# A new order of heads and filler in the mixer of a two-layer encoder, values by token tile, and inverse roots by one polynomial

## The chip, the cores and the metric

The kernel runs on one core of a Trainium2 chip. The metric is device time in microseconds (us) of one execution. Three runs of the kernel before took 1954.21, 1957.28 and 1953.86 us; the median is 1954.21 us.

## The reference

A trunk of two layers works on one sequence of 512 tokens with 1024 features. Each layer is a half-step SwiGLU, a token mixer, and another half-step SwiGLU; each is entered through an RMS norm with a learned shift and scale, and added to the residual through a gate. The change lies in the mixer (and in the helper for inverse roots, which all norms use):

```python
def token_mixing(h, cos, sin, w_in, sink, onorm_a, onorm_b, w_out):
    qa, ka, va, qb, kb, vb = jnp.split(h @ w_in, IN_SPLITS, axis=-1)
    qa, ka, qb, kb = (apply_rope(t, cos, sin) for t in (qa, ka, qb, kb))
    oa, _ = banded_attention(qa, ka, va, 128, sink)       # 8 heads, 2 key/value heads, |i-j| <= 128
    for window, dilation in ((128, 1), (512, 4), (2048, 16)):
        o, l = dilated_branch(qb, kb, vb, window, dilation)   # 8 heads, merged by their denominators
        ...
    ya = rmsnorm(oa, onorm_a)
    yb = rmsnorm(ob, onorm_b)
    return jnp.concatenate([ya, yb], axis=-1) @ w_out
```

All is float32, and the kernel keeps that precision: each operand is held as a high part and a low part, and a product is three TensorE matmuls (high by high, high by low, low by high).

## The kernel before, in words

Features lie on the 128 partitions and the 512 tokens in the free dimension. Weights come in chunks of 128x1024 (512 KB): `emit_chunk` loads one (L148), ScalarE makes its high part (L152) and VectorE its low part (L153). `chunk` hands over the next chunk, and `ahead` keeps three loaded beyond it.

**Sixteen heads.** The mixer has 8 heads of kind B (masked, all 512 keys for each tile of 128 queries) and 8 of kind A (a band, 256 or 384 keys). Two heads are a pair, since they share one 128-row projection. b0 to b3 and a0 to a3 are the pairs. Every pair has its own query projection; each B pair has its own keys, and all A pairs share one key projection, `ka`. Values of all heads are made in two halves of 320 columns by `vproj`.

**A head's work.** `scores(qt)` makes a tile of scores with two matmuls (L690, L691), adds the mask and takes the row extreme on VectorE (L695), and takes the exponential on ScalarE (L699). The result is a buffer `sm`, of which there are five. `pv(kt)` transposes one key tile of the probabilities on TensorE (L724), makes high and low parts (L727 on ScalarE, L728 on VectorE) and multiplies by the values (L731, L732) into the PSUM tile `po`. `finish` brings `po` to SBUF (L741 ScalarE, L742 VectorE); for the second head of a pair it also transposes the denominators (L746, tile `pd`), multiplies them in (L747) and adds the squares for the branch's norm. `heads_` goes through the heads: while it does the four `pv` of one head it issues the four `scores` of the next, so a head is four steps and a fifth for `finish`. Five steps stand ahead of the first head.

**Filler.** `weave` draws other TensorE work into these steps. Before the change the filler is first `fill_b`: both halves of the values, then nine projections (`proj`: 24 matmuls of 512 columns, then `rope`) in the order q, k of b2, q, k of b3, ka, and the four qa. Each step draws 1.62 us of it (FB; in the code's own reckoning a projection is 5.2 us and half of the values 13.1 us). Head 10 and later draw 0.45 us per step (FA) from `fill_a`: the conversion of the four normed B tiles (`conv`, L792 to L794) and the B half of the output projection (eight jobs of 12 matmuls, each with a residual addition, L391). What is left of a filler is drawn at its end.

**`rope`** reads a projection's PSUM tile twice on VectorE (L605, L606), goes through GpSimd (L607), adds (L608), makes the high part on ScalarE (L609) and the low part on GpSimd (L611), and moves the result into place with four DMAs for a query and eight for a key, all in SP's queue. Its temporaries `part`, `t1` and `qh` have one buffer each, so the next `rope` has to wait until these DMAs have read them. Queries go to `qs` (two buffers), keys to `kh` and `kl` (two buffers each).

**PSUM** has eight tiles of 128x512: four of tag `mm` (projections, values, `po`, `pd`), two for scores, two of tag `pt` (transposes, statistics).

**The norm of branch B.** `bb.stat` sums the squares of the B heads on TensorE (L774) and takes the inverse root on VectorE (`rsqrt`, L232 to L238: ten small operations, each on the one before). `bb.bcast` spreads the root by four transposes (`pRo`, L782) and a copy (L786); the filler `fill_a` needs it. HJ places `stat` at the first step of head 9 and `bcast` at its fourth. The norm of branch A follows all heads.

**Order on the engines.** The program is traced in the order told here, and the framework that builds it orders each engine's instructions once, at build time, by readiness and a priority that goes by place in the trace. `high_priority(offset=...)` moves an instruction ahead by so many places: heads by 50 (HB) up to head 7, by 150 (HA) after. That order is part of the program.

Of the kernel before, what the change touches and what calls it, by code (L numbers as in the profile page):

```python
# [1 line left out]

# [15 lines left out]
L = 2  # L18
# [13 lines left out]
RA, RB, RQ = 10.0 / 3, 5.0, 9.0 / 64  # L32
RK = (8.0 / 3) ** 12
# [14 lines left out]
HJ = [(9, 0), (9, 3)]  # L48
HN = 10
# [5 lines left out]
FB = 1.62  # L55
FA = 0.45
# [7 lines left out]
def tile_trunk(ctx: ExitStack, tc: tile.TileContext, xT, c, positions, adaT, cols, sink, wi1, wo1,  # L64
# [44 lines left out]
    for l in range(L):  # L109
        for sub, (wi, wo) in enumerate(((wi1, wo1), (None, None), (wi2, wo2))):  # L110
            finer.update(range(len(specs) - 3, len(specs) + 6))
            if wi is None:
                for j in (0, 1, 2, 3):
                    specs.append(wqk[l, j])
                for a in range(2):
                    for k0, n in ((0, 3), (3, 3), (6, 2)):
                        specs.append(wv[l, a][:, k0 * 320:(k0 + n) * 320])
                for j in range(4, 13):
                    specs.append(wqk[l, j])
# [472 lines left out]
    def mixer(l, norm, pool, mod):  # L592
# [8 lines left out]
        def rope(p, kind):  # L601
# [12 lines left out]
            if kind == "q":  # L614
# [7 lines left out]
            kh = pool.tile([128, 2, S], F32R, tag="kh", name="kh", bufs=2)  # L622
            kl = pool.tile([128, 2, S], F32R, tag="kl", name="kl", bufs=2)
# [7 lines left out]
        def proj(kind, dst):  # L631
# [5 lines left out]
            dst.append(rope(p, kind))  # L637
            ahead()

        def vproj():  # L640
            for _ in range(4):
                V2.append(pool.tile([128, 10, 2, 64], F32R, tag=f"v{len(V2)}", name="v2"))
            for a in range(2):
                ps = [pm.tile([128, S], F32, tag="mm", name="mm") for _ in range(4)]
                for k0, n in ((0, 3), (3, 3), (6, 2)):
                    W = chunk()
                    for tt in range(4):
                        for j in range(n):
                            k = k0 + j
                            ts = slice(tt * 128, tt * 128 + 128)  # L650
                            o = ps[tt][:, :320]
                            wh, wl = (w[:, j * 320:(j + 1) * 320] for w in W)
                            hh, hl = norm.h[k]
                            T.matmul(o, hh[:, ts], wh, start=k == 0, stop=False)  # L654
                            T.matmul(o, hh[:, ts], wl, start=False, stop=False)
                            T.matmul(o, hl[:, ts], wh, start=False, stop=k == KD - 1)
                            yield 0.41
                    ahead()
                for tt in range(4):
                    src = ps[tt][:, :320].rearrange("p (h d) -> p h d", d=64)  # L660
                    dst = V2[tt][:, 5 * a:5 * a + 5]
                    with tc.high_priority(offset=HP):
                        A.activation(dst[:, :, 0, :], src, AF.Copy)
                        V.tensor_tensor(dst[:, :, 1, :], src, V2[tt].bitcast(F32)[:, 5 * a:5 * a + 5, 0, :],
                                        op=ALU.subtract)
                vdone.append(a)

        two, halves = [], []

        class Head:  # L670
# [160 lines left out]
        def weave(main, fills):  # L831

            due = 0.0
            i = 0
            for n in main:
                if i + 1 < len(fills) and n >= fills[i + 1][0]:
                    for _ in fills[i][1]:
                        pass
                    i += 1
                    due = 0.0  # L840
                due += fills[i][2]
                while due > 0:
                    d = next(fills[i][1], None)
                    if d is None:
                        break
                    due -= d
            for _ in fills[i][1]:
                pass

        kinds = "qkqk"  # L850
        st = []
        for j, p in enumerate(group(norm, gs, sh, 4)):
            st.append(rope(p, kinds[j]))
        def fill_b():
            yield from vproj()
            for kind in "qkqkkqqqq":
                yield from proj(kind, st)
# [3 lines left out]
        def need(n):  # L861
            while len(st) < n:
                next(fb)

        def head_b(i, a):
            def f():
                need(2 * i + 2)
# [309 lines left out]
```

## Time and profile before

| | us |
|---|---|
| median of 3 runs | 1954.21 |
| lowest and highest | 1953.86, 1957.28 |
| the profiled execution, its own time | 1957.33 |
| its span, from first to last instruction | 1955.5 |
| TensorE busy | 1910.5 (98%) |
| VectorE busy | 1521.8 (78%) |
| ScalarE busy | 943.0 (48%) |
| mean granted TensorE clock | 0.993 |

The span is what the trace covers; the execution's own time has 1.8 us around it. A busy TensorE is not one at its peak, since ends of matmuls are modelled, so where its speed matters the spacing of starts is read. The two mixers lie at about 380 to 650 us and 1330 to 1600 us.

### The profile page before, as it was taken

To read this page: it belongs to the slowest core of one execution; us is meant where nothing else is said; L and a number is where in the kernel's file an instruction comes from. 1 tells how busy PE (TensorE), PEld (TensorE's weight loads), DVE (VectorE), ACT (ScalarE), POOL (GpSimd) and SP (SyncE) were. 2 spreads that over 40 slices of the span, in tenths; PEclk is the share of its full clock that TensorE was granted. 3 is DMA by queue.
4 is the path that set the end of the run, shared out by engine and by line. 5 is a ranking of instruction groups with operands and counts; after the bars stand their busy time and mean duration, and the time that the engine had idled before them with its cause. 6 is when DMAs were issued, how large, how long until landed. Compare 5 with 4: busy or idle time off the path is not lost.

```text
span 1955.5 us, 31018 instructions
## 1 busy us (share of the span) xinstructions
PE 1910.5 (98%) x12000; PEld 1713.5 (88%) x12000; DVE 1521.8 (78%) x2687; ACT 943.0 (48%) x1782; POOL 86.5 (4%) x63
## 2 busy tenths in 40 slices
PE   7999999999989999999999999999999999999998
PEld 5788888898768998989999898999977799898998
DVE  8868384477888988899688898867778889686773
ACT  5422222246665553536446363553657656353552
POOL 2000000011210000000000000000222000000000
PEclk8999999999989999999999999999999999999999
DMA  7778384244521155463414645342543113333231
GB/s 273 281 270 308 122 290 152 76 127 124 129 66 54 55 165 196 147 206 129 150 58 151 204 135 167 108 130 73 157 114 103 38 50 106 100 105 120 80 117 44
DMA packets 84678, 267.96 MB, mean 137 GB/s; under 512 B 10673, under 2 KB 13361, under 8 KB 84530
## 3 DMA queue, kind: packets, MB, share of 16 engines
q1 hardware_dynamic: 84530, 265.98, 42.5%
q8 instruction: 94, 1.54, 0.3%
q14 instruction: 54, 0.44, 0.1%
HBM read 244.97 MB, written 2.10 MB: 126 GB/s over the span
## 4 chain that ended last, share of the span: by engine, by line
PE 86%; DVE 6%; ACT 3%; DMA 2%; issue 2%; POOL 0%; SPq 0%; DVEq 0%; ACTq 0%; POOLq 0%
PE mm L221 16%; PE mm L222 16%; PE mm L223 16%; PE mm L483 9%; PE mm L484 9%; PE mm L485 9%; PE ptr L724 2%; PE po L731 1%; DVE araw L315 1%; PE po L732 1%; DMA araw<-in_adaT_dram 1%; PE s L690 1%; PE s L691 1%; ACT sm L699 1%; PE mm L654 1%
## 5 line engine op out<-in xcount | busy, mean ns | idle before, releaser
L152 ACT ACTIVATE hi<-raw 128x512 fp32r<-128x512 f32 (+5 forms) x253 | 215.1, 865 | 296.9 <-PE mm L223 204.0
L153 DVE TENSOR_TENSOR lo<-raw,hi 128x512 fp32r<-128x512 f32 (+5 forms) x253 | 258.7, 1032 | 88.0 <-ACT hi L152 86.7
L221 PE MATMUL mm<-hh,hi 128*128 128x512 f32 (+1 forms) x864 | 306.6, 356 | 8.0 <-ACT hh L293 7.7
L223 PE MATMUL mm<-hl,hi 128*128 128x512 f32 (+1 forms) x864 | 303.0, 356 | 2.9 <-DVE hl L294 2.9
L222 PE MATMUL mm<-hh,lo 128*128 128x512 f32 (+1 forms) x864 | 305.3, 355 | 0.5 <-DVE lo L990 0.4
L222 PE MATMUL mm<-gh,lo 128*128 128x512 f32 (+1 forms) x832 | 297.0, 357 | 0.0
L221 PE MATMUL mm<-gh,hi 128*128 128x512 f32 (+1 forms) x832 | 296.8, 357 | 0.0
L223 PE MATMUL mm<-gl,hi 128*128 128x512 f32 (+1 forms) x832 | 296.5, 356 | 0.0
L483 PE MATMUL mm<-sh,hi 128*128 128x256 f32 x912 | 260.2, 285 | 1.2 <-ACT sc L505 0.7
L484 PE MATMUL mm<-sh,lo 128*128 128x256 f32 x912 | 258.2, 283 | 0.0
L485 PE MATMUL mm<-sl,hi 128*128 128x256 f32 x912 | 258.0, 283 | 0.0
L180 ACT ACTIVATE hi<-raw 128x512 fp32r<-128x512 f32 x228 | 132.3, 623 | 141.4 <-issue 73.4
L221 PEld LDWEIGHTS mm<-hh,hi 128*128 128x128 f32 x864 | 164.2, 190 | 30.8 <-ACT hh L293 9.4
L391 DVE SCALAR_TENSOR_TENSOR x<-mm,fin,x 128x512 f32<-128x512 f32 (+1 forms) x156 | 101.7, 654 | 112.4 <-PE mm L223 112.0
L223 PEld LDWEIGHTS mm<-hl,hi 128*128 128x128 f32 x864 | 163.1, 190 | 26.2 <-DVE hl L294 5.1
L222 PEld LDWEIGHTS mm<-hh,lo 128*128 128x128 f32 x864 | 163.8, 190 | 22.6 <-DVE lo L990 1.8
L223 PEld LDWEIGHTS mm<-gl,hi 128*128 128x128 f32 x832 | 157.2, 189 | 22.6
L222 PEld LDWEIGHTS mm<-gh,lo 128*128 128x128 f32 x832 | 157.3, 189 | 22.3
L221 PEld LDWEIGHTS mm<-gh,hi 128*128 128x128 f32 x832 | 157.2, 189 | 22.2
L483 PEld LDWEIGHTS mm<-sh,hi 128*128 128x128 f32 x912 | 173.9, 191 | 2.0 <-ACT sc L505 0.9
L484 PEld LDWEIGHTS mm<-sh,lo 128*128 128x128 f32 x912 | 174.2, 191 | 0.0
L485 PEld LDWEIGHTS mm<-sl,hi 128*128 128x128 f32 x912 | 174.1, 191 | 0.0
(185 smaller groups left out, 4016.4 us busy)
## 6 DMA issues: line engine op xcount, KB each, us to landing
raw<-in_wi_dram SPq DMA_DIRECT2D x171, 512.0 KB, 3.7
araw<-in_adaT_dram SPq DMA_DIRECT2D x144, 512.0 KB, 4.6
raw<-in_wo_dram SPq DMA_DIRECT2D x64, 448.0 KB, 3.9
raw<-in_wo_dram SPq DMA_DIRECT2D x32, 512.0 KB, 3.6
raw<-in_wqk_dram SPq DMA_DIRECT2D x26, 512.0 KB, 3.9
raw<-in_w_out_dram SPq DMA_DIRECT2D x16, 512.0 KB, 3.7
kh<-qh SPq DMA_DIRECT2D x40, 128.0 KB, 2.3
kl<-t SPq DMA_DIRECT2D x40, 128.0 KB, 2.3
```

Of the source, the lines that this page charges most:

```text
L152: A.activation(hi[:, sl], raw[:, sl], AF.Copy)
L153: V.tensor_tensor(lo[:, sl], raw[:, sl], hi.bitcast(F32)[:, sl], op=ALU.subtract)
L180: A.activation(d, r, AF.Copy)
L221: T.matmul(ps, wh, X[0][:, s], start=start, stop=False)
L222: T.matmul(ps, wl, X[0][:, s], start=False, stop=False)
L223: T.matmul(ps, wh, X[1][:, s], start=False, stop=stop)
L315: return V.tensor_tensor_reduce(out=raw, in0=raw, in1=by, scale=1.0, scalar=0.0, op0=ALU.mult, op1=ALU.add, accum_out=mod[:, l, ch, k:k + ...
L391: ins = V.scalar_tensor_tensor(x[:, m, s], ps[:, s], gate[:, m:m + 1], x[:, m, s], op0=ALU.mult, op1=ALU.add).ins
L483: T.matmul(ps, wh, xh, start=start and k == 0, stop=False, skip_group_check=True)
L484: T.matmul(ps, wl, xh, start=False, stop=False, skip_group_check=True)
L485: T.matmul(ps, wh, xl, start=False, stop=stop and k == 3, skip_group_check=True)
L724: T.transpose(p[:, j * 128:j * 128 + 128], self.sm[qt][:, c0:c0 + 128], ident)
```

## The change

Heads come in the order b0 b1 a0 b2 b3 a1 a2 a3. The filler is one chain: half 0 of the values, ka, qa0, qb2, kb2, half 1 of the values, qb3, kb3, qa1, qa2, qa3, and behind them `fill_a`, which yields nothing to do until `bb.R` is there. A step draws 2.7 us up to head 5, 0.75 us from head 6, 0.85 us from head 10. `stat` moves to the last step of head 10 and `bcast` to the third step of head 11. A half of the values is made token tile by token tile, in one PSUM tile at a time, with its three chunks fetched at its start; the columns of the weights are regrouped so that half 0 serves b0, b1 and a0. Keys have one buffer of each of two tags instead of two of one: kb0 and ka share the first, kb1, kb2 and kb3 the second. HB holds up to head 9. `rsqrt` has one cubic polynomial instead of two steps: eight operations instead of ten.

```diff
+PAIRS = ("b0", "b1", "a0", "b2", "b3", "a1", "a2", "a3")
+FILL = ("v0", "ka", "qa0", "qb2", "kb2", "v1", "qb3", "kb3", "qa1", "qa2", "qa3")
-HJ = [(9, 0), (9, 3)]
-HN = 10
+HJ = [(10, 3), (11, 2)]
+RATES = ((0, 2.7), (6, 0.75), (10, 0.85))
-FB = 1.62
-FA = 0.45
...
-        for ca, cb, o in ((RA, RB, y), (RA / RQ, RB / RQ ** 2, out)):
-            V.tensor_tensor(t, y, y, op=ALU.mult)
-            V.tensor_tensor(t, t, v, op=ALU.mult)
-            V.scalar_tensor_tensor(q, t, -ca, t, op0=ALU.add, op1=ALU.mult)
-            last = V.scalar_tensor_tensor(o, q, cb, y, op0=ALU.add, op1=ALU.mult).ins
+        V.tensor_tensor(t, y, y, op=ALU.mult)
+        V.tensor_tensor(t, t, v, op=ALU.mult)
+        for i, ca in enumerate(RC):
+            o, u = (out, y) if i == 3 else (q, t)
+            last = V.scalar_tensor_tensor(o, q if i else t, ca, u, op0=ALU.add, op1=ALU.mult).ins
...
-            kh = pool.tile([128, 2, S], F32R, tag="kh", name="kh", bufs=2)
-            kl = pool.tile([128, 2, S], F32R, tag="kl", name="kl", bufs=2)
+            j = kind in ("kb1", "kb2", "kb3")
+            kh = pool.tile([128, 2, S], F32R, tag=f"kh{j:d}", name="kh")
+            kl = pool.tile([128, 2, S], F32R, tag=f"kl{j:d}", name="kl")
...
+        def vproj(a):
+            Ws = []
+            for k0, n in VK:
+                W = chunk()
+                Ws += [(W, j) for j in range(n)]
+            for tt in range(4):
+                p = pm.tile([128, S], F32, tag="mm", name="mm")
+                for k, (W, j) in enumerate(Ws):
...
+                vdone.append((a, tt))
...
             def pv(self, kt):
+                while (self.vh // 5, kt) not in vdone:
+                    next(fb)
                 if kt == 0:
-                    while len(vdone) < self.vh // 5 + 1:
-                        next(fb)
...
-                with tc.high_priority(offset=hp[0] if n < 8 else hp[1]):
+                with tc.high_priority(offset=hp[0] if n < 10 else hp[1]):
...
         def fill_a():
+            while not hasattr(bb, "R"):
+                yield None
...
+        weave(heads([head(t, a) for t in PAIRS for a in range(2)], (HB, HA), {HJ[0]: bb.stat, HJ[1]: bb.bcast}),
+              chain(fb, fill_a()), RATES)
```

## Rows read from the trace of the kernel before

**Rows 1.** The page: busy time of TensorE, share, instructions.

```profile
PE 1910.5 (98%) x12000; PEld 1713.5 (88%) x12000; DVE 1521.8 (78%) x2687; ACT 943.0 (48%) x1782; POOL 86.5 (4%) x63
```

**Rows 2.** Stretches of layer 0's mixer: us, busy PE, PEld, DVE, ACT, POOL, clock, DMA.

```profile
430.00:556.00 126.00, 124.74 (x666) 102.34 (x665) 100.75 (x205) 82.82 (x171) 26.32 (x19) 1.00 0.42 116
556.00:568.00 12.00, 5.66 (x37) 4.43 (x37) 11.05 (x32) 7.27 (x19) 3.05 (x2) 0.90 0.11 27
568.00:576.00 8.00, 8.00 (x30) 6.84 (x31) 4.78 (x14) 3.94 (x10) 0.00 (x0) 0.50 0.39 110
576.00:600.00 24.00, 21.62 (x121) 16.55 (x120) 21.40 (x66) 21.14 (x63) 0.00 (x0) 1.00 0.03 7
```

**Rows 3.** The same view of layer 1's mixer, around its stall.

```profile
1505.00:1518.00 13.00, 6.66 (x42) 5.27 (x41) 11.36 (x33) 7.85 (x19) 3.12 (x3) 0.87 0.17 41
1518.00:1522.00 4.00, 4.00 (x17) 3.13 (x17) 2.14 (x5) 1.94 (x5) 0.00 (x0) 0.57 0.36 122
```

**Rows 4.** Timeline, TensorE: start, us, engine, line, instruction, idle before it.

```profile
567.91 0.45 PE L782 MATMUL pRo<-ident,y 128*128 128x128 f32 x1 [6.03 <-DVE y L238]
```

**Rows 5.** Timeline, VectorE, in the same stall.

```profile
564.48 0.69 DVE L153 TENSOR_TENSOR lo<-raw,hi 128x512 fp32r<-128x512 f32 x1
...
567.41 0.16 DVE L237 SCALAR_TENSOR_TENSOR r<-r 128x4 f32<-128x4 f32 x1
567.61 0.16 DVE L238 SCALAR_TENSOR_TENSOR y<-r,r 128x4 f32<-128x4 f32 x1
```

**Rows 6.** Timeline, ScalarE: ends of A heads behind the stall.

```profile
576.10 0.59 ACT L741 ACTIVATE y<-po 64x512 f32<-64x512 f32 x1 [1.05 <-PE po L732]
...
593.00 0.59 ACT L741 ACTIVATE y<-po 64x512 f32<-64x512 f32 x1
```

**Rows 7.** Timeline, TensorE: first matmuls of the values and of branch A's output.

```profile
419.95 0.31 PE L654 MATMUL mm<-hi,hh 128*128 128x320 f32 x1
...
623.84 0.39 PE L221 MATMUL mm<-yah,hi 128*128 128x512 f32 x1
```

**Rows 8.** Dense stretches, columns as rows 2: 256-column and 512-column matmuls.

```profile
1640.00:1650.00 10.00, 10.00 (x86) 10.00 (x85) 10.00 (x16) 6.37 (x13) 0.00 (x0) 1.00 0.41 119
1690.00:1700.00 10.00, 10.00 (x46) 8.29 (x45) 6.24 (x9) 2.32 (x5) 0.00 (x0) 1.00 0.29 94
```

**Rows 9.** Timeline, TensorE: eight transposes of probabilities in a row.

```profile
541.33 1.04 PE L724 MATMUL ptr<-ident,sm 128*128 128x128 f32 x8
```

**Rows 10.** VectorE groups by shape, 418 to 616 us: count, busy us, mean ns, idle.

```profile
L695 DVE CUSTOM_DVE_ANT_0 sm<-s,mask 128x512 f32<-128x512 f32 x32 | 21.5, 687 | 5.2 <-PE s L691 4.9
L728 DVE TENSOR_TENSOR pl<-ptr,ph 128x512 fp32r<-128x512 f32 x32 | 21.3, 685 | 3.1 <-ACT ph L727 2.9
L742 DVE TENSOR_TENSOR y<-po,y 64x512 f32<-64x512 f32 x16 | 11.0, 688 | 6.4 <-ACT y L741 6.2
L695 DVE CUSTOM_DVE_ANT_0 sm<-s,mask,nsnk 128x384 f32<-128x384 f32 x16 | 9.6, 611 | 0.2 <-PE ptr L724 0.2
L605 DVE STREAM_SHUFFLE part<-mm 128x512 f32<-128x512 f32 x12 | 8.9, 745 | 0.0
L728 DVE TENSOR_TENSOR pl<-ptr,ph 128x384 fp32r<-128x384 f32 x16 | 8.8, 549 | 1.8 <-ACT ph L727 1.7
L608 DVE TENSOR_TENSOR t<-t,part 128x512 f32<-128x512 f32 x12 | 8.2, 686 | 0.2
...
L695 DVE CUSTOM_DVE_ANT_0 sm<-s,mask,nsnk 128x256 f32<-128x256 f32 x16 | 7.3, 478 | 0.6 <-PE s L691 0.5
L728 DVE TENSOR_TENSOR pl<-ptr,ph 128x256 fp32r<-128x256 f32 x16 | 6.7, 417 | 2.9 <-ACT ph L727 2.8
```

**Rows 11.** ScalarE groups by shape, same stretch.

```profile
L699 ACT ACTIVATE sm<-sm,nb 128x512 f32<-128x512 f32 x32 | 23.0, 719 | 13.3 <-DVE nb L695 13.3
L727 ACT ACTIVATE ph<-ptr 128x512 fp32r<-128x512 f32 x32 | 18.3, 594 | 6.1 <-PE ptr L724 5.7
...
L699 ACT ACTIVATION_READ_ACCUMULATOR sm<-sm,nb 128x1 f32 x64 | 12.1, 189 | 0.0
```

More of the change, by code (lines that the diff above doesn't have):

```diff
@@ L1 @@
 from contextlib import ExitStack, nullcontext
+from itertools import chain
 import numpy as np
@@ L112, in tile_trunk @@
             if wi is None:
[L113 to L119, printed above, removed]
+                specs += [wqk[l, QK.index(t)] for t in FIRST]
+                for t in FILL:
+                    if t[0] == "v":
+                        for k0, n in VK:
+                            specs.append(wv[l, int(t[1])][:, k0 * 320:(k0 + n) * 320])
+                    else:
+                        specs.append(wqk[l, QK.index(t)])
                 for half in (1, 0):
@@ L629, in rope, with proj @@
             return kh, kl
-        def proj(kind, dst):
+        def proj(kind):
             W = chunk()
@@ L636, in proj @@
                 yield 0.65
-            dst.append(rope(p, kind))
+            st[kind] = rope(p, kind)
             ahead()
[L640 to L657, printed above, removed]
-                    ahead()
[L659 to L666, printed above, removed]
@@ L668, in mixer @@
-        two, halves = [], []
+        def vproj(a):
+            if not V2:
+                V2.extend(pool.tile([128, 10, 2, 64], F32R, tag=f"v{tt}", name="v2") for tt in range(4))
+            Ws = []
+            for k0, n in VK:
+                W = chunk()
+                Ws += [(W, j) for j in range(n)]
+            for tt in range(4):
+                ts = slice(tt * 128, tt * 128 + 128)
+                p = pm.tile([128, S], F32, tag="mm", name="mm")
+                o = p[:, :320]
+                for k, (W, j) in enumerate(Ws):
+                    wh, wl = (w[:, j * 320:(j + 1) * 320] for w in W)
+                    hh, hl = norm.h[k]
+                    T.matmul(o, hh[:, ts], wh, start=k == 0, stop=False)
+                    T.matmul(o, hh[:, ts], wl, start=False, stop=False)
+                    T.matmul(o, hl[:, ts], wh, start=False, stop=k == KD - 1)
+                    yield 0.44
+                src = o.rearrange("p (h d) -> p h d", d=64)
+                dst = V2[tt][:, 5 * a:5 * a + 5]
+                with tc.high_priority(offset=HP):
+                    A.activation(dst[:, :, 0, :], src, AF.Copy)
+                    V.tensor_tensor(dst[:, :, 1, :], src, V2[tt].bitcast(F32)[:, 5 * a:5 * a + 5, 0, :],
+                                    op=ALU.subtract)
+                vdone.append((a, tt))
+                if tt < 3:
+                    ahead()
+            ahead()
@@ L670, in mixer @@
+        two = []
         class Head:
@@ L829, in heads_, with weave, head @@
                 cur = nxt
-        def weave(main, fills):
+        def weave(main, fill, rates):
             due = 0.0
-            i = 0
             for n in main:
[L836 to L841, printed above, removed]
+                due += [r for h, r in rates if n >= h][-1]
                 while due > 0:
-                    d = next(fills[i][1], None)
+                    d = next(fill, None)
                     if d is None:
+                        due = 0.0
                         break
                     due -= d
-            for _ in fills[i][1]:
+            for _ in fill:
                 pass
[L850 to L853, printed above, removed]
+        st = {}
+        for t, p in zip(FIRST, group(norm, gs, sh, 4)):
+            st[t] = rope(p, t)
         def fill_b():
-            yield from vproj()
-            for kind in "qkqkkqqqq":
-                yield from proj(kind, st)
+            for t in FILL:
+                yield from vproj(int(t[1])) if t[0] == "v" else proj(t)
         fb = fill_b()
[L861 to L865, printed above, removed]
+        def head(t, a):
             def f():
-                need(2 * i + 2)
-                return Head(st[2 * i], a, st[2 * i + 1], a, 2 + 2 * i + a, bb, False, None)
+                i = int(t[1])
+                h = 2 * i + a
+                kind, vh = ("kb%d" % i, h + h // 4) if t[0] == "b" else ("ka", 4 + 5 * (i // 2))
+                for need in ("q" + t, kind):
+                    while need not in st:
+                        next(fb)
+                if t[0] == "b":
+                    return Head(st["q" + t], a, st[kind], a, vh, bb, False, None)
+                return Head(st["q" + t], a, st[kind], i // 2, vh, ba, True, l * 8 + h)
             return f
@@ L914, in fill_a @@
                 ahead()
-        weave(heads([head_b(i, a) for i in range(4) for a in range(2)] +
-                    [head_a(i, a) for i in range(4) for a in range(2)], (HB, HA), {HJ[0]: bb.stat, HJ[1]: bb.bcast}),
-              ((0, fb, FB), (HN, fill_a(), FA)))
+        weave(heads([head(t, a) for t in PAIRS for a in range(2)], (HB, HA), {HJ[0]: bb.stat, HJ[1]: bb.bcast}),
+              chain(fb, fill_a()), RATES)
         nxt = Norm()
```

22 lines of the change are left out of this document (11 added, 11 removed).

## The prediction

> **What bounds the kernel now.** I read the page first, then the stretches of the two mixers, then the timeline at the one deep gap, then the groups by shape. The page [rows 1] says that TensorE is busy 98% of the span: a change in order can win only where TensorE waits, or runs slowly, inside the mixers. The stretches of layer 0 [rows 2] show where. From 430 to 556 us, while heads and filler run together, TensorE is busy 124.7 of 126 us and VectorE 100.8: TensorE bounds. From 556 to 568 TensorE is busy 5.7 of 12 us, and the next 8 us run at a granted clock of 0.50 (1.2 of 2.4 GHz). From 576 to 600 only heads run and little filler: VectorE is busy 21.4 of 24 us (89%), so VectorE bounds here, and TensorE waits in small pieces. Layer 1 repeats this with about 4 us at a clock of 0.57 [rows 3].
>
> The timeline names the deep gap: TensorE stood 6.03 us in front of `pRo`, the spreading of the B norm's root [rows 4]. VectorE was not idle; it did the root's small operations between 0.69 us ones of the backlog [rows 5]. In that order nothing behind `pRo` can go ahead.
>
> Behind the gap, the end of one A head and that of the third one after it lie 16.9 us apart [rows 6]: **5.63 us for an A head without much filler.**
>
> **The change part by part.** I price the stage from the first matmul of the values, 419.95 us, to the first of branch A's output, 623.84 us [rows 7]: 203.9 us in layer 0.
>
> *TensorE's prices.* Dense stretches give 10/86 = 0.116 us for a matmul of 256 columns and 10/46 = 0.217 for 512 [rows 8]; between them 0.142 for 320 and 0.167 for 384 columns are estimates on that line. A transpose is 1.04/8 = 0.13 us [rows 9]. So a projection (24 matmuls) is 5.2 us, both halves of the values (192) 27.2, a B head (16 matmuls of 512, 18 transposes) 5.8, an A head (8 of 384, 8 of 256, 12 transposes) 3.8, and the B half of the output projection (96) 20.9. Before, the filled part lasted from 419.95 to about 556.6 us and held the values, nine projections, eight B heads and two A heads: 27.2 + 46.8 + 46.4 + 7.6 = 128 us of work in 136.7, a factor of 1.07 that I keep.
>
> *Order and rates.* The old rate draws 73 us of filler (in the code's reckoning) at 1.62 a step, 5 of them early for the first `pv`; it is used up near step 42, in the last B head. The new one draws 75 us at 2.7 a step: used up at step 28, in the first head of a0. Nothing more can be drawn until `bcast` at step 63, since `fill_a` waits for the root; the rate of 0.75 draws nothing. I split the stage there.
>
> - Part one, filled: values 27.2, eight of the nine projections 41.6 (the ninth has no PSUM tile until a rope is freed), four B heads 23.2, half an A head 1.9 and scores of the next 0.6: 94.5 x 1.07 = **101 us**, bound by TensorE.
> - Part two, steps 28 to 63: three A heads' worth and the four B heads b2, b3, bound by VectorE. An A head is 5.63. A B head has more VectorE work: four score tiles at 687 and four low parts at 685 ns against two each at 611, 478, 549 and 417 [rows 10], 5.49 less 4.11 = 1.38 us, so 7.0. Its bounds: below, TensorE's own 5.8 x 1.07 = 6.2; above, 7.9, the chain through the five `sm` buffers. In a B head all four `sm` are read until the last `pv`, so three of the next head's scores can only follow: 3 x 0.687, an exponential of 0.719 + 0.189 [rows 11], four transposes 0.5, a high part 0.594, two low parts 1.37, four transposes 0.5, the `finish` addition 0.69 [rows 10], and 0.2 at each of six changes of engine (an estimate, from the 0.2 us between dependent small operations, rows 5), 7.8 to 7.9. I take 7.0, nearest the measured pace of heads. Four ropes fall here too, 0.745 + 2 x 0.686 = 2.1 us of VectorE each, 8.5; bounds 0 (in TensorE's shade) and 8.5; I take 8.5, as VectorE bounds. 16.9 + 28.0 + 8.5 = **53.4 us.**
> - Part three: four and a half A heads 17.2, the output projection 20.9, two statistics of some 32 transposes and one-column matmuls 4.2: 42.3 x 1.07 = **45 us**, bound by TensorE; VectorE has some 25 us of heads and 16 of conversions and additions beside it.
>
> Sum 199.4, so 4.5 us less than 203.9. In layer 1 the old stage lost 1.7 us to the half clock (0.43 of 4) against 4.0 (0.50 of 8), so 2.2 us less there. Together **-6.7 us.**
>
> For the split of regimes the stretches show 100.8 of 126 us of VectorE in the filled part and 21.4 of 24 in the unfilled one [rows 2]. The Trainium skill (Perfetto Trace Analysis, Optimization Strategy) advises to interleave regimes in which different engines are contended. By it a filler drawn sooner lengthens the unmixed part and gives nothing, so that only the roots below would be won; by my rows the mix of the third part pays for the second.
>
> *The stall.* `stat` to `bcast` was three steps and is seven, some 9 us of heads, against the 6.03 us missed [rows 4]. I cost the wait at nothing because these heads hide it. If that cover is gone the price is 6 us a layer. VectorE stays late then, in any case.
>
> *Roots.* Two operations less, 0.2 us apart [rows 5]: 0.4 us each, on the path at the kernel's first norm and its last, **-0.8 us**; the others lie beside matmuls. They also end 0.4 us sooner at `pRo`, within the cover above.
>
> *Values by token tile.* The same 192 matmuls, eight additions and ScalarE copies. Its three chunks must be there within the first 18 matmuls, 2.5 us, instead of 10; `ahead` has loaded them beside the four first projections. Bounds 0 and 2.5 us a layer; I take 0. The gain, that `pv` waits for one tile, has its worth in part one, which TensorE bounds: 0.
>
> *Keys' buffers, and SP's queue.* The number of DMAs is the same. The keys of b3 now wait for the last scores of b2, at step 39, and hold `t1` and `qh`; three projections wait behind them in three of the four `mm` tiles, and `po` and `pd` share the last one. Queued behind: ropes on VectorE, and on SP the copies of qa1. What waits for these is a1, three heads later. Bounds 0 and four hand-overs of the last PSUM tile, 0.59 [rows 6] + 0.69 [rows 10] = 1.28 us each, 5.1 a layer; I take 0, since most of it would fall where VectorE has other work. The regrouped weights cost nothing on the chip.
>
> Total -7.5 us. The profiled execution took 1957.33 us, its span of 1955.5 and 1.8 around it; it becomes 1949.8. The profiled one is 3.1 above the median of 1954.21, so against the median the same difference gives **1947 us**.
>
> **The rivals.** *One, slower: buffers bind in part two.* From step 28 on, B heads run at the `sm` chain's 7.9 us and each `po` waits for the last PSUM tile. 4 x 0.9 + 5.1 = 8.7 us a layer, 17.4 in all: 1964 us. It outweighs the gain from 3.7 us a layer on, and makes the kernel measurably slower from 5.7. For it: nothing in the trace shows a B head without filler, and three held tiles follow from the code. Against it: A heads kept VectorE 89% busy [rows 2]. The same page of the Trainium skill and section says that repeated equal gaps on the engine that should be full can mean that SBUF or PSUM has no room for the next tile; that is this rival, and by it the time is the one just given. No gap of that kind is in the trace before.
>
> *Two: the stall comes back.* The order is fixed at build time, and VectorE is again behind it when `pRo` stands in TensorE's line. 2 x 6.0 us: 1959 us. For it: VectorE is the later engine all through part two. Against it: four steps more.
>
> *Three: more is won.* The ropes of part two hide after all: 8.5 us a layer, 1930 us. For it: VectorE's sums count operations that overlap at their edges. Against it: VectorE at 89%.
>
> **How the numbers follow.** My forecast has 0.42, rival one 0.28, two 0.13, three 0.17. A measurement of this kernel can tell about 0.2%, 3.9 us, from no change. Faster by more: 0.85 of the forecast's share (its takings of 0 could eat 4 us) and all of three, 0.53. Within: the rest of the forecast, a fifth of one and under half of two, 0.17. Slower: 0.30. Cases of both signs hold much; the forecast's own range is 1940 to 1952 (part two's B heads at 6.2 or 7.6). The range of 1930 to 1966 reaches to rivals three and one; what lies beyond either is under 2 in 10.
>
> **What would show it.** Right: no wait over 2 us of `pRo` for VectorE; no stretch at a clock of 0.5 in the mixers; filler's `mm<-hh` matmuls gone some 105 us into the stage; then about 53 us with TensorE some 80% and VectorE 90% busy; the stage at 199 us. Rival one: TensorE and VectorE both below 85% there, and ends of B heads about 8 us apart or more. Rival two: `pRo` with an idle of 4 us or more. I would be wrong altogether if the filler's end stays near 130 us into the stage, for then the rates do not set its place, or if the time changes outside the mixers.

## The result, and the profile after

The changed kernel takes 1967.95 us (median of four runs, 1966.8 to 1969.93) against 1954.03 us: a ratio of 1.0069, with a 95% interval of 1.0051 to 1.0086. It is slower, where a gain of 7.5 us had been forecast, and the time lies 2 us above the upper end of the range.

The page of the profile has TensorE's busy share as before, 98% [rows 1]; the two VectorE operations less in each root show in VectorE's count, 2,653 for 2,687:

```profile
PE 1920.0 (98%) x12000; PEld 1716.6 (87%) x12000; DVE 1517.0 (77%) x2653; ACT 940.7 (48%) x1782; POOL 87.2 (4%) x63
```

The stage that the prediction priced runs, in layer 0, between these two rows of TensorE's timeline (they answer to [rows 7]): 210.9 us where it was 203.9.

```profile
418.05 0.31 PE L661 MATMUL mm<-hi,hh 128*128 128x320 f32 x1
...
628.94 0.50 PE L226 MATMUL mm<-yah,hi 128*128 128x512 f32 x1 [0.35 <-ACT yah L801]
```

In layer 1 it grew by 9.4 us, from 201.2 (1370.9 to 1572.0) to 210.5 (1374.1 to 1584.7). The first of the two stages starts 1.9 us earlier than before, and what lies between them takes another 1.8 us less, so that the end of the second comes 12.6 us later: all but 0.1 of what the spans differ by (1968.2 against 1955.5). Nothing is lost outside the mixers.

Now the stage, cut at the same places in both kernels: its first 20 us, then to the last filler matmul of high part by high part (`mm<-hh,hi`), then to `pRo`, then to the end. The view of stretches, columns as in [rows 2]; first the kernel before:

```profile
419.90:439.90 20.00, 19.27 (x124) 17.92 (x123) 10.57 (x23) 9.15 (x18) 5.83 (x5) 1.00 0.54 158
439.90:555.60 115.70, 114.44 (x601) 92.73 (x600) 93.65 (x190) 75.08 (x156) 24.21 (x18) 1.00 0.45 123
555.60:568.00 12.40, 6.06 (x39) 4.79 (x38) 11.05 (x32) 7.67 (x19) 3.05 (x2) 0.91 0.14 33
568.00:623.80 55.80, 53.39 (x274) 43.05 (x275) 45.06 (x118) 36.10 (x93) 0.00 (x0) 0.93 0.16 47
```

and the changed kernel, with its layer 1 between filler and `pRo` as the last row:

```profile
418.00:438.00 20.00, 20.00 (x127) 18.70 (x126) 13.21 (x26) 10.57 (x21) 5.53 (x5) 1.00 0.59 153
438.00:537.00 99.00, 97.15 (x507) 79.45 (x506) 70.49 (x143) 54.89 (x113) 20.97 (x14) 1.00 0.43 123
537.00:583.00 46.00, 37.49 (x174) 26.49 (x172) 37.85 (x97) 33.43 (x81) 6.33 (x5) 0.90 0.28 69
583.00:628.90 45.90, 42.90 (x230) 34.32 (x230) 37.50 (x94) 27.10 (x70) 0.00 (x0) 0.99 0.11 35
...
1492.70:1538.90 46.20, 37.56 (x174) 26.59 (x174) 37.93 (x97) 33.50 (x81) 6.32 (x5) 0.90 0.28 69
```

The counts in brackets (x) are the key. Both stages hold the same 1,038 TensorE instructions (matmuls and transposes; matmuls for short below); what differs is the company in which they pass. Beside filler they pass at 725/135.7 = 5.34 per us before and 634/119 = 5.33 after. Without filler, 174 of them take 46 us: 3.78 per us. Before, only 39 stood there, with the stall among them. That these 174 are other instructions is not the reason: from the very last filler matmul (538.69 us) to `pRo` the timeline has 44 matmuls of 512 columns, 20 of 384, 20 of 256 and 84 transposes and sums, 26 us of work at the prediction's prices, and they take 44.5 us, 1.7 times as long; beside filler the factor is 1.08 (112 us of work in 120.6). Behind `pRo`, where the output projection fills in, it is 274/55.8 = 4.91 before and 230/45.9 = 5.01 after. So the filled part shrank by 16.7 us, the last part by 9.9, and the stretch between them grew by 33.6: 7.0 more.

The old stall is gone. `pRo` waits 0.35 us where it waited 6.03 [rows 4]:

```profile
583.15 0.45 PE L790 MATMUL pRo<-ident,y 128*128 128x128 f32 x1 [0.35 <-DVE y L243]
```

What took its place is no single wait. In the middle of the unfilled stretch no engine is full (TensorE 29.9 of 38 us, some of it at half the clock, VectorE 30.7, ScalarE 26.8), and the view of waits lists TensorE's losses in the whole stage, each as total, times, longest:

```profile
546.00:584.00 38.00, 29.93 (x139) 21.65 (x139) 30.72 (x85) 26.75 (x67) 6.33 (x5) 0.87 0.19 45
...
PE s L698 <- DVE nb L703: 2.7, 3, 2.1
PE po L739 <- ACT ph L735: 2.3, 5, 1.0
PE pso L782 <- DVE acco L776: 2.1, 1, 2.1
PE ptr L732 <- DVE pl L736: 2.1, 5, 0.9
```

But for `pso`, the sums of the norm, these are waits in the loop of one head: scores, row extreme, exponential, transpose, high and low part, product. The longest of these waits shows one way in which it comes about: the matmul has its keys and queries, but has to wait for one of the two PSUM tiles for scores until VectorE has read it. VectorE's timeline, and that matmul:

```profile
545.67 0.68 DVE L703 CUSTOM_DVE_ANT_0 sm<-s,mask 128x512 f32<-128x512 f32 x1
...
546.28 0.69 DVE L613 TENSOR_TENSOR t<-t,part 128x512 f32<-128x512 f32 x1
...
547.00 0.69 DVE L750 TENSOR_TENSOR y<-po,y 64x512 f32<-64x512 f32 x1
...
547.73 0.73 DVE L610 STREAM_SHUFFLE part<-mm 128x512 f32<-128x512 f32 x1
...
548.49 0.69 DVE L755 TENSOR_TENSOR y<-y,pd 128x512 f32<-128x512 f32 x1
...
549.10 0.68 DVE L703 CUSTOM_DVE_ANT_0 sm<-s,mask 128x512 f32<-128x512 f32 x1
...
549.85 0.80 PE L698 MATMUL s<-kh,qs 128*128 128x512 f32 x1 [2.14 <-DVE nb L703]
```

Two operations of ropes (L613, L610) and two of a finished pair (L750, L755) stand between two row extremes, 3.4 us apart, and TensorE has no filler to spend the time on. ScalarE's rows of L749 show where heads end: the sixth head, the two of b2, the two of b3, which come 13.3 and 8.7 us after one another, and the two of a1, the second of which has `pso` and `pRo` in it and comes 11.3 us after the first:

```profile
533.50 0.59 ACT L749 ACTIVATE y<-po 64x512 f32<-64x512 f32 x1
541.03 0.59 ACT L749 ACTIVATE y<-po 64x512 f32<-64x512 f32 x1
545.75 0.59 ACT L749 ACTIVATE y<-po 64x512 f32<-64x512 f32 x1 [1.32 <-PE po L740]
559.09 0.59 ACT L749 ACTIVATE y<-po 64x512 f32<-64x512 f32 x1 [0.41 <-PE po L740]
567.79 0.59 ACT L749 ACTIVATE y<-po 64x512 f32<-64x512 f32 x1
574.44 0.59 ACT L749 ACTIVATE y<-po 64x512 f32<-64x512 f32 x1
585.78 0.59 ACT L749 ACTIVATE y<-po 64x512 f32<-64x512 f32 x1 [0.20 <-PE po L740]
```

### The profile page after: what moved, and what is told of

It is laid out like the page before. It is cut to its first block, busy times and chain, and to the rows that moved or that the text cites. A ratio compares the mean times of both kernels' runs of the same rounds, so it can differ in the third digit from the quotient of the medians.

```text
span 1968.2 us, 30999 instructions
## 1 busy us (share of the span) xinstructions
PE 1920.0 (98%) x12000; PEld 1716.6 (87%) x12000; DVE 1517.0 (77%) x2653; ACT 940.7 (48%) x1782; POOL 87.2 (4%) x63
## 4 chain that ended last, share of the span: by engine, by line
PE 87%; DVE 6%; ACT 4%; issue 1%; DMA 1%; POOL 0%; SPq 0%; DVEq 0%; ACTq 0%; POOLq 0%
PE mm L226 17%; PE mm L227 16%; PE mm L228 16%; PE mm L488 10%; PE mm L489 9%; PE mm L490 9%; PE ptr L732 2%; PE po L739 1%; PE po L740 1%; PE s L698 1%; ACT sm L707 1%; PE mm L662 1%; PE mm L661 1%; PE mm L663 1%; PE s L699 1%
## 5 line engine op out<-in xcount | busy, mean ns | idle before, releaser
L228 PEld LDWEIGHTS mm<-gl,hi 128*128 128x128 f32 x832 | 157.2, 189 | 22.7
```

Of the source, the lines that this page charges most:

```text
L228: T.matmul(ps, wh, X[1][:, s], start=False, stop=stop)
```

## The experiments

Twelve kernels were run, each timed beside the kernel before. This table has eight of them with the two kernels of the prediction, read from the views of stretches of layer 0. "With filler" reaches to the last `mm<-hh,hi` matmul and holds the first 20 us; "without" goes on to `pRo`. The filler's last two matmuls follow within 1.8 us, in the last row of the table only 3.3 and 3.8 us later, so that some 44 of its 64 are without any filler.

| kernel | TensorE busy in the first 20 us | with filler: us, instructions | without: us, instructions | behind `pRo`: us, instructions | stage |
|---|---|---|---|---|---|
| before (rate 1.62) | 19.3 | 135.7, 725 | 12.4, 39 | 55.8, 274 | 203.9 |
| before at 2.7 | 19.6 | 125.2, 651 | 31.8, 112 | 54.8, 274 | 211.8 |
| before, values by token tile | 17.3 | 140.2, 725 | 16.2, 39 | 55.2, 275 | 211.6 |
| the same, waiting for a half | 19.6 | 137.3, 727 | 12.2, 38 | 55.1, 274 | 204.6 |
| after (rate 2.7) | 20.0 | 119.0, 634 | 46.0, 174 | 45.9, 230 | 210.9 |
| after at 1.62 | 18.3 | 144.3, 767 | 14.0, 40 | 45.4, 230 | 203.7 |
| after at 1.3 | 16.6 | 151.0, 762 | 15.0, 46 | 46.5, 231 | 212.5 |
| after at 2.7, then 1.45 | 19.1 | 128.9, 693 | 27.0, 115 | 46.7, 230 | 202.6 |
| after at 1.62, waiting for a half | 20.0 | 132.4, 724 | 22.7, 85 | 45.4, 231 | 200.5 |
| after at 1.3, waiting for a half | 20.0 | 137.5, 745 | 17.9, 64 | 45.5, 231 | 200.9 |

### The old rate in the new order

```diff
-RATES = ((0, 2.7), (6, 0.75), (10, 0.85))
+RATES = ((0, 1.62), (10, 0.85))
```

> The changed kernel with the old drawing rate, 1.62 us a step instead of 2.7 up to head 9. Theory 1 (the filler is used up too early, and the heads behind it expose their own chain): the filler lasts to about step 46 of 63, the stretch without filler shrinks from some 46 us to some 25 us a layer, and the kernel takes 1948 to 1957 us. Theory 2 (too few buffers for scores) and theory 3 (one key buffer, and projections that hold PSUM tiles): the filler's place matters little, 1963 to 1970 us.

Measured: 1958.42 us, ratio 1.0018 (1.0008 to 1.0027). The view of stretches for the filled part, the unfilled one and the last:

```profile
440.00:564.30 124.30, 122.27 (x662) 100.27 (x661) 97.99 (x205) 80.95 (x171) 22.83 (x17) 1.00 0.42 115
564.30:578.30 14.00, 8.98 (x40) 7.24 (x39) 11.40 (x34) 9.07 (x23) 2.54 (x2) 0.76 0.26 76
578.30:623.70 45.40, 42.54 (x230) 33.92 (x230) 37.53 (x93) 27.12 (x70) 0.00 (x0) 1.00 0.11 36
```

The rate decides how many matmuls are left without cover: 40 for 174. That is worth some 10 us of the time, and turns the loss nearly into a draw. The time lies 1.4 us above the range given, and the stretch without filler shrank to 14 us where 25 had been expected. It doesn't yet make a gain: the first 20 us now have TensorE busy for 18.3 only, and `pso` waits 3.73 us for VectorE's sums (2.09 in the changed kernel).

### More buffers for the heads

Two kernels ask whether buffers bound the unfilled stretch, as rival one had it. The first has eight `sm` in place of five (the room comes from letting the spread root share `part` and the last A pairs' outputs share those of B); the second gives b3's keys tiles of their own, from the ring of the weights' high and low parts.

```diff
-s = pool.tile([128, S], F32, tag="sm", name="sm", bufs=5)
+s = pool.tile([128, S], F32, tag="sm", name="sm", bufs=8)
...
```

> The changed kernel with eight buffers for scores instead of five (paid for by sharing three tiles that are dead by then). Theory 2: the three scores that had to follow a B head's last transposes can run sooner, 4 to 6 us less a layer, 1956 to 1961 us. Theories 1 and 3: at most 2 us less a layer, 1964 to 1969 us.

```diff
+if kind == "kb3":
+    kh, kl = (wp.tile([128, 1024], F32R, tag=t, name=n).rearrange("p (a s) -> p a s", s=S)
+              for t, n in (("hi", "kh"), ("lo", "kl")))
...
```

> The changed kernel with key tiles of their own for b3, taken from the weights' pool. Theory 3: b3's keys no longer wait for b2's last scores, the ropes behind them free their PSUM tiles sooner, 3 to 5 us less a layer, 1958 to 1963 us. Theories 1 and 2: 1965 to 1969 us.

Measured: 1969.48 us, ratio 1.0074 (1.0059 to 1.0089), and 1975.62 us, ratio 1.0109 (1.0094 to 1.0124). The unfilled stretch of the first, and of the second:

```profile
534.80:580.50 45.70, 36.77 (x181) 27.00 (x180) 38.92 (x105) 34.70 (x88) 6.34 (x5) 0.93 0.29 70
```

```profile
545.60:588.20 42.60, 34.35 (x156) 24.10 (x154) 36.93 (x93) 30.89 (x74) 3.79 (x3) 0.88 0.31 90
```

Eight `sm` pass 181 matmuls in 45.7 us, 3.96 per us where five passed 3.78, and the time is the same. The keys' own tiles pass 156 in 42.6 us, 3.66 per us, and the filled part holds more stalls (103.4 busy of the 107 us behind the first 20), so that the whole is slower than any of the theories had it; that tiles taken from the weights' ring have a price of their own is likely and was not told apart. Neither buffer, as given here, makes the kernel faster. PSUM, with all eight tiles in use, was not tried, and the wait of 2.14 us above is one for a PSUM tile.

### The new root alone

The kernel before with the one polynomial in `rsqrt`, as in the diff of the change.

> The kernel before with the new inverse root alone. My sum says 0.8 us less, 1953.2 us. If the deep gap at the B norm's root is shortened too by the two operations in VectorE's queue, up to 2 us a layer less, 1949 us. If the new order that the shorter root gives at build time is worse, some us more.

Measured: 1953.39 us, ratio 1.0002 (0.9991 to 1.0013). The 0.8 us that was forecast can't be told from nothing, and the stall at `pRo` is nearly what it was (5.62 us against 6.03).

### The values alone

The kernel before with `vproj` by token tile, the wait per tile in `pv` and the regrouped columns, in the old order and at the old rate.

> The kernel before with the values made token tile by token tile (and the weights regrouped for it), nothing else. If the filler's place is what costs, this part is free: 1954 us within 3. If fetching three chunks at once or the single PSUM tile stalls TensorE, 3 us or more slower; if heads that start sooner help, 2 to 5 us faster.

Measured: 1971.62 us, ratio 1.0088 (1.007 to 1.0106). The part costed at nothing is by itself as slow as the whole change. Its stretches:

```profile
420.00:440.00 20.00, 17.30 (x101) 14.34 (x100) 10.33 (x25) 9.21 (x19) 6.19 (x5) 1.00 0.60 172
440.00:560.20 120.20, 118.34 (x624) 95.73 (x624) 94.83 (x186) 74.32 (x153) 24.73 (x17) 1.00 0.42 116
560.20:576.40 16.20, 8.67 (x39) 7.16 (x38) 12.97 (x34) 7.76 (x19) 2.87 (x2) 0.71 0.20 55
576.40:631.60 55.20, 53.31 (x275) 42.70 (x275) 45.36 (x118) 35.93 (x93) 0.00 (x0) 0.93 0.13 39
```

The loss starts in the first row: 101 matmuls in the first 20 us where the kernel before passes 124. TensorE waits there for the first heads' softmax (for row extremes, which free the tiles for scores, and for a high part), in this view of waits over the same 20 us:

```profile
PE s L693 <- DVE nb L698: 1.7, 2, 1.2
PE po L734 <- ACT ph L730: 0.6, 1, 0.6
```

Before, the first `pv` drew the whole half of the values into the program ahead of its own work, and this hid the first two heads. With the wait per tile the program lets that `pv` go ahead after a quarter of them. The 23 matmuls that are missing here are made up later, and push all that follows: of the 7.7 us that the stage is longer, 4.5 lie beside filler and 3.8 between filler and `pRo`, where the granted clock is 0.71 for 0.91.

### Thinner filler, and a later statistic

```diff
-RATES = ((0, 2.7), (6, 0.75), (10, 0.85))
+RATES = ((0, 1.3), (10, 0.85))
```

> The changed kernel at 1.3 us a step, so that the filler lasts to step 58 of 63. Theory 1 (filler used up too early): at least as good as 1.62 (1958.4), 1950 to 1957 us. Rival: at 1.62 what is left is not the filler but TensorE's wait in front of the B norm's sums, then this one stays within 3 us of 1958.4.

The next run has in addition `HJ = [(11, 1), (12, 0)]`, which moves `stat` and `bcast` by three steps.

> As the run at 1.3 us a step, and the B norm's sums and root three steps later (head 11, step 2; head 12, step 1). If TensorE's wait in front of the sums is what is left, 3 to 6 us less a layer than the run at 1.3. If the output projection locked behind the root matters more, some 3 us a layer more.

Measured: 1976.43 us, ratio 1.0104 (1.0081 to 1.0128), and 1977.54 us, ratio 1.0116 (1.0101 to 1.0131). Only 46 matmuls are left without filler at 1.3, and yet it is slower than at 2.7. Its start and its filled part show why:

```profile
419.00:439.00 20.00, 16.59 (x81) 13.13 (x80) 12.00 (x25) 9.10 (x18) 5.42 (x5) 0.83 0.58 152
439.00:570.00 131.00, 126.97 (x681) 103.20 (x680) 98.65 (x201) 80.22 (x169) 21.89 (x17) 1.00 0.39 109
```

81 matmuls pass in the first 20 us against 127, partly at the half clock (granted 0.83). The largest wait in them is not for the softmax; the view of waits has it first:

```profile
PE s L699 <- DMA kl<-t: 2.0, 1, 2.0
```

At this rate the first scores come before the DMA that brings the keys' low parts into place has landed, and the 7 us behind this wait, 429.3 to 436.3 us, pass at a granted clock of 0.52. The idea that a later end of the filler is better in itself fell with this run: a thin filler loses at the start more than it saves at the end. The later statistic brought nothing beside it.

### The new rate in the old order

```diff
-FB = 1.62
+FB = 2.7
```

> The kernel before, in its old order, with its filler drawn at 2.7 us a step instead of 1.62. Theory 1: the filler ends some 15 steps sooner and the B heads behind it have no cover, 8 to 16 us slower, 1962 to 1970 us. If the new order of pairs is the cause and the rate only in it, within 3 us of 1954.

Measured: 1975.09 us, ratio 1.0103 (1.0086 to 1.0121). Some 20 us are lost by this one number, with no part of the change in the kernel, where 8 to 16 had been expected. The stretch between filler and `pRo`:

```profile
544.50:576.30 31.80, 22.50 (x112) 16.87 (x111) 27.91 (x77) 22.79 (x59) 6.80 (x5) 0.89 0.20 50
```

112 matmuls in 31.8 us, 3.52 per us, though a wait of 4.18 us at `pRo` is among them. The slow passage belongs to heads without filler in the old order too. VectorE is fuller here, 27.9 of 31.8 us (88%), than in the changed kernel.

### The start and the end told apart

From here on the theory was that the stage wants a full start and a filler that reaches near `pRo`. Three kernels: the changed one at 2.7 for the first pair and 1.45 then; the kernel before with the new values but the old wait; and the changed one at 1.62 with the old wait. The first edit below is the first kernel's; the second is that of the other two, against the run of the values alone and against the changed kernel at 1.62.

```diff
-RATES = ((0, 2.7), (6, 0.75), (10, 0.85))
+RATES = ((0, 2.7), (2, 1.45), (10, 0.85))
```

> The changed kernel with a filler rate of 2.7 for the first pair of heads, 1.45 from then to head 10, 0.85 after. Theory (the stage takes as long as its matmuls, some 1,038 of them, which pass at 5.3 per us beside filler and at under 4 without; the first 20 us want a high rate, the rest a filler that reaches head 10): TensorE full in the first 20 us as in the changed kernel (20.0 busy there, against 18.3 at a rate of 1.62), filler gone about 140 to 146 us into the stage, stage 200 to 202 us, time 1950 to 1954. Rival (only the place of the filler's end counts, and 1.62 was already there): 1957 to 1960, as at 1.62. Rival two (a filler spread thinly starves the heads whatever the start): 1970 or more, as at 1.3.

```diff
-while (self.vh // 5, kt) not in vdone:
+while (self.vh // 5, 3) not in vdone:
```

> The kernel before with the values by token tile, as in the run that cost 17 us, but a head's first product waits for all four tiles of its half again, as it did before. Theory (the wait per tile is what costs there: the first heads no longer draw the whole half of the values ahead of their own work, so that TensorE waits for the softmax in the first 20 us and all later filler comes later): TensorE busy 19.3 or more in the first 20 us of the stage (17.3 with the wait per tile), stage 204 to 206 us, time 1954 to 1960. Rival (the values' own order costs: three weight chunks fetched at once, one PSUM tile for each token tile, columns of B ahead of those of A): 1968 to 1972, unchanged.

> The changed kernel at a rate of 1.62 and with the wait for all four value tiles of a half. Theory: the first 20 us of each mixer are full again (19.3 busy or more against 18.3), which takes 2 to 3 us off each layer of the run at 1.62: 1952 to 1955. Rival (the wait per tile has no part in it in this order): 1957 to 1960, as at 1.62 with the wait per tile.

Measured, in this order: 1951.01 us, ratio 0.9988 (0.9979 to 0.9998); 1958.76 us, ratio 1.0025 (1.0015 to 1.0034); 1948.19 us, ratio 0.9968 (0.9955 to 0.998). The middle one's start:

```profile
415.90:435.90 20.00, 19.55 (x129) 18.39 (x127) 10.19 (x25) 8.98 (x18) 6.22 (x5) 1.00 0.59 172
```

The last one's four stretches:

```profile
419.50:439.50 20.00, 20.00 (x128) 18.82 (x127) 12.65 (x25) 10.57 (x20) 5.47 (x5) 1.00 0.58 153
439.50:551.90 112.40, 110.36 (x596) 91.20 (x595) 90.53 (x187) 71.56 (x153) 22.70 (x17) 1.00 0.46 126
551.90:574.60 22.70, 18.46 (x85) 14.24 (x84) 18.36 (x53) 16.01 (x42) 2.56 (x2) 0.77 0.20 53
574.60:620.00 45.40, 42.57 (x231) 33.94 (x231) 37.53 (x93) 27.21 (x70) 0.00 (x0) 1.00 0.11 36
```

In all three the time went the way of the theory and not of its rivals. The wait per tile is most of what the values cost (1.0088 became 1.0025); the rest, some 5 us, is not placed: in the profiled executions the stages are 0.7 and 2.8 us longer than before, and these executions, 1955.13 us here and 1957.33 before, are the fastest of the one kernel and the slowest of the other. The first kernel's filler ended earlier than expected, 128.9 us into the stage for 140 to 146, and its stage was 202.6 us for 200 to 202; the time was inside. The last kernel took 4 us less than the range given: with the whole half drawn at the start, its heads run 85 matmuls without filler at 3.74 per us, and its stage is 3.2 us shorter than at 1.62 with the wait per tile.

The last two differ in the order of pairs and of filler, with its rate behind head 10, its statistic's place, its heads' priority and its key buffers, and in the root, and agree in the rate of 1.62, the values and the wait: 1958.76 against 1948.19. **The new order, with all that goes with it, is worth about 10 us**, once its filler lasts. By the table it is won beside filler: 724 matmuls in 132.4 us for 727 in 137.3. What stands behind the filler's end takes as long as before, 316 in 68.1 us for 312 in 67.3: the last part gives 9.7 us with 43 matmuls less, and the stretch without filler takes 10.5 more with 47 more.

### Thinner still, with a full start

```diff
-RATES = ((0, 2.7), (6, 0.75), (10, 0.85))
+RATES = ((0, 1.3), (10, 0.85))
...
-while (self.vh // 5, kt) not in vdone:
+while (self.vh // 5, 3) not in vdone:
```

> As the run at 1.62 with the wait for all four value tiles (1948.2 us), at a rate of 1.3. Theory: what made 1.3 slow with the wait per tile was the empty first 20 us of each mixer (16.6 busy) and what it put off, and the wait for the whole half fills them whatever the rate; the filler then ends later than 132 us into the stage and fewer than 85 matmuls pass without it: stage 197 to 201 us, time 1944 to 1950. Rival (1.3 is too thin at any start: heads run ahead and TensorE waits for the softmax between): filler gone 140 us or later into the stage all the same, stage 204 us or more, time 1956 or more.

Measured: 1953.25 us, ratio 0.9995 (0.9986 to 1.0004). The start is full at 1.3 too (20.0 busy, against 16.6 with the wait per tile), the time 23 us below that of the same rate without this line, and the stage of layer 0 as forecast. The time is 3 us above the range given, and 5 us above that at 1.62; the stage of layer 1 has most of this, 203.1 us for 199.2. The matmuls without filler fell to 64, but the waits for VectorE at the statistic grew; two rows of TensorE's timeline:

```profile
566.01 0.56 PE L782 MATMUL pso<-ones,acco 128*128 128x1 f32 x2 [3.37 <-DVE acco L776]
...
574.27 0.30 PE L790 MATMUL pRo<-ident,y 128*128 128x128 f32 x1 [1.50 <-DVE y L243]
```

At 1.62 these are 2.09 and 0.50 us. It looks as if less uncovered work brings the statistic closer behind the heads, so that the old stall begins to come back; no run tried a later statistic here.

## Why the prediction was wrong

**What bounds the kernel: right for the filled part, wrong for the unfilled one.** TensorE bounds beside filler, and its prices there, with the factor of 1.07, held: 5.33 matmuls per us against 5.34. But the reading of 576 to 600 us, that VectorE bounds there with 21.4 of 24 us, was carried over to heads of kind B with ropes among them. There VectorE is busy 30.7 of 38 us, 81%, and TensorE 79%: no engine's sum of durations gives the time, and what TensorE's idle time holds is waits of a head's loop. (Even in the old stretch 23 of TensorE's 121 instructions, `mm<-yh` and `mm<-yl`, are filler.)

**Part one, 101 us forecast, 119 measured: the place of the end.** The filler is used up at step 28 in the order of the trace, but the engines don't work in that order. The likely reason is that heads stand ahead by 50 places; at 537 us six heads had ended, and the seventh ended at 541, where four and a half had been counted. With the ninth projection and two more heads the same prices give 27.2 + 46.8 + 23.2 (four heads of B) + 7.6 (two of A) and most of another B head, 5.8: 110.6 x 1.07 = 118. So the price was right and the list of what lies in the stretch was not. For the stage this is no loss by itself, since the same work was taken out of part two.

**Part two: the step that failed.** The two parts were put at 101 + 53.4 = 154.4 us together and took 119 + 46 = 165. Of the 53.4 us, what was in fact done inside the filled part came to some 20 (a B head 7.0, one and a half A heads 8.4, two ropes 4.2), which leaves 34 us by the prediction's prices for what took 46. Two terms failed. The first was mis-sized: the B head without filler, put at 7.0 us with 7.9 as its upper bound. The two heads of b3 took 22.0 us, with two ropes, where 18.2 had been priced (2 x 7.0 and 2 x 2.1), so 8.9 each with the rope taken off. The bound of 7.9 was a chain through the `sm` buffers that left out two things seen in the longest wait: the two PSUM tiles for scores, and what VectorE's own order puts between two row extremes. How much each of these and the half clock take of the 3.8 us is open; no run took the ropes out of the stretch or gave scores a third tile.

The second term was put at nothing: the statistic, which heads were to hide. The second head of a1 took 11.3 us where 5.63 had been priced. The waits of 2.09 us at `pso` (the third of the four rows of waits above) and 0.35 at `pRo` and some 3 us of half clock behind the first (an estimate, half of the 6.29 us that TensorE was busy there) make up about all of these 5.7 us. The two terms together are 9.5 of the 12 us; the rest is not placed. TensorE at the half clock, which the prediction had expected nowhere in the mixers, shows in two stretches of the changed kernel:

```profile
549.60:553.00 3.40, 3.15 (x10) 2.47 (x10) 2.72 (x8) 2.56 (x7) 0.71 (x1) 0.50 0.50 118
576.90:583.80 6.90, 6.29 (x28) 5.62 (x27) 3.82 (x15) 3.29 (x8) 0.00 (x0) 0.51 0.00 0
```

These 10.3 us are as many as before, where 8 us at 0.50 and 12 us at 0.90, which makes 2.4 us at the half clock, stood around the stall [rows 2]: the stall went and its half clock did not. (The 2.2 us by which the prediction let layer 1 lose less to the clock are 2.3, 4.0 less 1.7; in the changed kernel the two layers lose the same.) The first follows the wait of 2.14 us at 549.85, the second that at `pso`.

**Part three, 45 us forecast, 45.9 measured: right.**

**The stall: gone as forecast, but not by the cover that was counted, so partly by luck.** 0.35 us were left of 6.03. The prediction counted seven steps between `stat` and `bcast`, some 9 us of heads. By its own reckoning of five steps a head there are four, one more than before, and from the first `pso` to `pRo` only 6.7 us passed (10.8 before). What changed is the root: its operations took VectorE from 558.37 to 567.77 us before, 9.4 us, with those of a rope, of a finished pair and of weights' low parts between them, and 4.7 us now, with those of heads alone between them. VectorE did not stay late, as the prediction had it. The first operation of the root before, then the first and the last of the changed kernel:

```profile
558.37 0.16 DVE L232 TENSOR_SCALAR r<-pso 128x4 f32<-128x4 f32 x1 [0.15 <-PE pso L774]
...
578.32 0.16 DVE L237 TENSOR_SCALAR r<-pso 128x4 f32<-128x4 f32 x1 [1.97 <-PE pso L782]
...
582.84 0.16 DVE L243 SCALAR_TENSOR_TENSOR y<-r,r 128x4 f32<-128x4 f32 x1
```

**The roots: right within what can be told.** 0.8 us were forecast, and nothing can be measured.

**Values by token tile, costed at 0 with bounds of 0 and 2.5 us a layer: wrong as a single edit, and by luck near in the whole.** Alone, the edit costs 17 us. What the prediction weighed was the matmuls and the loads; what counts is how much `pv` draws ahead of itself. The changed kernel escapes the empty start only through its rate: at 2.7 its first 20 us are full, at 1.62 they are not. Rate and wait are tied: with the wait per tile the high rate is needed for the start, and costs more in the middle. Neither fault shows its own price while the other is there.

**Keys' buffers: nothing speaks against the 0**; the run with b3's own tiles gained nothing, though its tiles may have cost the weights something.

**The rivals.** Rival one came nearest, with 1964 us, and its marks appeared: both engines below 85%, B heads over 8 us apart. Of its mechanism one half did not show: eight `sm` changed nothing. Nor does the view of waits from 537 to 583 us list a wait of `po` for a freed tile. PSUM for scores and transposes, which the rival did not name, is another matter: of the 7.6 us of waits in that view, 2.4 are for a freed tile of scores and 1.3 for one of transposes. The Trainium skill (Perfetto Trace Analysis, Optimization Strategy) has equal gaps that repeat as a possible sign of too little room; the run with eight `sm` speaks against that for the `sm` tiles, and for the PSUM tiles of scores and transposes it stays open. Rivals two and three did not come: `pRo` waited 0.35 us, and nothing more was won. The other rule of the Trainium skill from the same section, that regimes with different contended engines be interleaved, was given only the roots' gain by the prediction. The runs at 2.7 agree with it, and go further: a filler drawn sooner, which lengthens the unmixed stretch, costs some 20 us in the old order and some 10 in the new one with the wait per tile. The prediction's own test, that it would be wrong altogether if the filler's end stayed near 130 us, was not the one that decided; the end came forward, and the stretch behind it was dearer than its engines' sums.

## What to carry to other kernels

Price a stretch without filler by how fast its instructions pass in a measured row of the same kind, not by the busiest engine's sum of durations, and where the trace has no such row, make one with a run (here the old order at the new rate). In ten kernels 1,037 to 1,040 TensorE instructions made up the stage; whether 40 or 174 of them passed at under 4 per us instead of 5.3 was worth some 10 us. It is not the only thing that counts: the values alone leave 39 without filler and the rate of 1.3 leaves 46, and both are as slow as the changed kernel or slower, by their starts. Where a rate and a data wait both set how far filler runs ahead, change and time them one at a time, since each can hide the other's cost. And keep the good half of such a change: with one line that waits for the whole half of the values, and the old rate, the new order takes 1948.19 us, 0.9968 (0.9955 to 0.998) of the kernel before, and beats both.

## What was not expected of the hardware

A thin start cost the clock as well: at a rate of 1.3 TensorE was busy 16.6 of its first 20 us and the granted clock of these was 0.83, where it was 1.00 at 2.7 (20.0 busy) and at 1.62 (18.3 busy). The low clock came behind one wait of 2.05 us for a DMA. And removing a stall of 6 us returned none of the half clock in layer 0 (10.3 us for 10.4): two waits of some 2 us each, within a stretch where TensorE was busy 79%, were followed by 3.4 and 6.9 us at 0.50 and 0.51.
